# HGRN2 mixer of a hybrid encoder layer: block steps skewed by one tile, values transposed with the projections

## The chip, the cores and the metric

The kernel runs on one core of a Trainium2 chip. The core has a matmul engine (PE, with its weight loads PEld), three engines for elementwise work (DVE, ACT, GpSimd, in the profile POOL), and a sequencer, SP, that issues most DMAs. The metric is the device time of one execution in microseconds.

## What is computed

One layer of an encoder for a prompt of 1024 tokens and a sample of 64, with the same weights: a wide input projection, four token mixers side by side (A mLSTM, B forgetting attention, C HGRN2, D RG-LRU), each with a gate and a branch projection, their sum, a layer norm and a gated convolutional feed-forward. The change is in mixer C alone, 4 heads with a 128x128 state:

```python
z = hg_f.astype(F32).reshape(bsz, t_len, HG_HEADS, HG_DK)
lbh = lb.reshape(HG_HEADS, HG_DK)
hg_logf = jnp.log(jnp.maximum(lbh + (1.0 - lbh) * jax.nn.sigmoid(z), TINY))
hg_k = (1.0 - lbh) * jax.nn.sigmoid(-z)
o_hg, hg_s = hgrn2_chunkwise(jax.nn.silu(hg_q)..., hg_k, hg_i..., hg_logf, hg_s)
y_hg = head_rms_norm(o_hg, hg_norm_g).astype(x.dtype) * jax.nn.silu(hg_g)

def hgrn2_chunkwise(q, k, v, logf, s0):
    # S_t = diag(f_t) S_{t-1} + k_t v_t^T, o_t = S_t^T q_t, by blocks
    def step(s, blk):
        bcum = jnp.cumsum(fc, axis=2)
        qe = qc * jnp.exp(bcum)
        a = jnp.where(causal, jnp.einsum('bhtk,bhsk->bhts', qe, kc * jnp.exp(-bcum)), 0.0)
        o = jnp.einsum('bhts,bhsv->bhtv', a, vc) + jnp.einsum('bhtk,bhkv->bhtv', qe, s)
        b_last = bcum[:, :, -1]
        s_new = jnp.exp(b_last)[..., None] * s + jnp.einsum(
            'bhsk,bhsv->bhkv', kc * jnp.exp(b_last[:, :, None] - bcum), vc)
        return s_new, o
```

## The kernel before

Activations lie with features on partitions and the 1088 tokens along the free axis, in three chunks of 384, 384 and 320 columns. A projection (`dense`, line 311) takes for each chunk one PSUM bank and 24 matmuls: `mm3` (line 293) runs three products for each of 8 slices of the inner dimension, since weights and inputs are split into a high and a low half. The weights come by DMA as `wr`; `wh` (ACT or GpSimd, lines 259 and 261) and `wl` (DVE, line 262) are made from it a little ahead of use. `bank` hands out PSUM banks by kind, two of each: "d" for the projections (in the profile psd), "m" for transposes and scores (psm), "s" for the products (pss). Whoever takes a bank waits until the engine that empties it is done.

Mixer C runs head by head, here called unit 0 to 3. `P_C(u)` makes the projections of a head: forget gate `z`, query `qc`, value `vT`, output gate `gs`, 12 chunks in all, each evicted by ACT (`qc` and `gs` with a pass on DVE behind). `M_C(u)` does the rest in three parts:

- The front (lines 892 to 949), on whole rows of 128x1088: on ACT the absolute value of `z` (892), exponentials (893, 896) and two logarithms (897, 898) with loads of ACT's function table between; on DVE lines 899, 901, 904 and 905 and a scan (907), `dd` (911); on ACT two exponentials (913, 914); on DVE `kc` (916, it has the place of `z`) and `qc` (915); on GpSimd `qR` (947) and `kU` (949). Small passes on the block sums make `EX`, `eR`, `eU` and `eT`.
- The transposes (line 957) of `vT` and then `kU`, nine tiles each in groups of 4, 4 and 1, through an "m" bank; `vt` is copied by DVE (961), `kt` by ACT (959). There is a yield after each group.
- Nine steps, one for each tile of 128 tokens (the last has 64). `scores(t+1)`: `KX` on DVE (984), four matmuls (989), the lower triangle copied to `am` on DVE (992). `flip(t)`: a transpose of `am` (997), copied to `at` on ACT (999). `outs(t)`: the products `at` x `vt` (1009), `qR` x state (1011), `kt` x `vt` (1012), then `ot` (DVE, 1013), its square `sq` (ACT, 1015) and the new state `St` (DVE, 1018 or 1020). `tail` transposes and gates finished outputs (966 to 974).

`branch` (line 1432) weaves the generators: M_C of unit u-1 with P_C of unit u, and M_C of unit 3 with the gate projections, in the proportion of their yields, 19 to 12:

```python
for u in range(1, n):
    weave(Mg(u - 1), nM, Pg(u), nP)
weave(Mg(n - 1), nM, gates(m, range(4)), 12)
```

That gives the order in which the program is written. A scheduler then sets the final order on each engine: it moves instructions forward where their operands allow, and each engine runs its list in that order and waits at the front of it. So the front of unit u+1 lies on ACT and DVE between the last four steps of unit u.

Of the kernel before, what the change touches and what calls it, by code (L numbers as in the profile page):

```python
# [13 lines left out]
AF = mybir.ActivationFunctionType  # L14
OP = mybir.AluOpType
# [4 lines left out]
P = 128  # L20
# [14 lines left out]
HG_F, HG_I, HG_Q, HG_G = 3088, 3600, 4112, 4624  # L35
# [28 lines left out]
def tw(tt):  # L64
    return P if tt < 8 else TS
# [3 lines left out]
def trunk_kernel(ctx: ExitStack, tc: tile.TileContext, I, O, dbg=None):  # L69
    nc = tc.nc  # L70
    PE, V, S, G, SP = nc.tensor, nc.vector, nc.scalar, nc.gpsimd, nc.sync
# [239 lines left out]
    def dense(key, evict, tag="d", order=(0, 1, 2), ahead=2):  # L311
        wh, wl = wget(key, ahead)
        for c in order:
            n0, n = CH[c]
            ps = bank(tag)
            mm3(ps[:, :n], [(wh[:, k, :], wl[:, k, :], xh[c][:, k, :], xl[c][:, k, :]) for k in range(8)])
            evict(c, n0, n, ps[:, :n])
            yield
# [144 lines left out]
    pt = bank("s", 1024)  # L463
# [12 lines left out]
    def bc(c0):  # L476
        return pk[:, bcol(c0):bcol(c0) + 1]
# [273 lines left out]
    st = {}  # L751
# [96 lines left out]
    ams = []  # L848

    def blk(t, n=34):  # L850
        return t.rearrange("p (a b) -> p a b", b=32)[:, 0:n, :]

    def P_C(u):
        z = slot(s="z")
        bf = bc(HG_F + u * P)

        def ev(c, n0, n, ps):
            S.activation(z[:, n0:n0 + n], ps, AF.Identity, bias=bf)
        yield from dense(("in", HG_F + u * P), ev)

        def silu2(dst, j):
            b, bh = bc(j + u * P), bsil[j][:, u:u + 1]

            def evs(c, n0, n, ps):
                t = small([P, 384], "sil", 2)
                S.activation(t[:, :n], ps, AF.Tanh, bias=bh, scale=0.5)
                S.activation(dst[:, n0:n0 + n], ps, AF.Identity, bias=b)
                V.scalar_tensor_tensor(dst[:, n0:n0 + n], t[:, :n], 1.0, dst[:, n0:n0 + n], OP.add, OP.mult)
            return evs
        qc = slot(s="qc")  # L870
        yield from dense(("in", HG_Q + u * P), silu2(qc, HG_Q))
        vT = slot(s="vT")
        bi = bc(HG_I + u * P)

        def evv(c, n0, n, ps):
            S.activation(vT[:, n0:n0 + n], ps, AF.Identity, bias=bi)
        yield from dense(("in", HG_I + u * P), evv)
        gs = slot(s="gs")
        yield from dense(("in", HG_G + u * P), silu2(gs, HG_G))
        st["C", u] = z, qc, vT, gs  # L880

    def M_C(u):
        z, qc, vT, gs = st.pop(("C", u))
# [16 lines left out]
        kc = z  # L900
# [29 lines left out]
        EX = small([P, 9, 4, 4], "EX", 2)  # L930
# [16 lines left out]
        G.tensor_tensor(blk(qR), blk(qc), eR[:, 0:34].unsqueeze(2).to_broadcast([P, 34, 32]), OP.mult)  # L947
        kU = slot(s="kU")
        G.tensor_tensor(blk(kU), blk(kc), eU[:, 0:34].unsqueeze(2).to_broadcast([P, 34, 32]), OP.mult)
        vt, kt = slot([P, 9, P], s="vt"), slot([P, 9, P], s="kt")  # L950
        for src, dst, eng in ((vT, vt, 0), (kU, kt, 1)):
            for g0, g1 in ((0, 4), (4, 8), (8, 9)):
                pt = bank("m")
                p3 = pt.rearrange("p (a b) -> p a b", b=P)
                w = tw(g0)
                for tt in range(g0, g1):
                    PE.transpose(p3[0:w, tt - g0, :], src[:, tt * P:tt * P + w], ident)
                if eng:
                    S.activation(dst[0:w, g0:g1, :], p3[0:w, 0:g1 - g0, :], AF.Copy)
                else:  # L960
                    V.tensor_copy(dst[0:w, g0:g1, :], p3[0:w, 0:g1 - g0, :])
                yield
        ot = slot([P, 9, P], s="ot")
        ss = small([P, 9], "ss", 2)
        St = None
# [9 lines left out]
            if g1 == NT:  # L975
                yput(2, u, gs)

        def scores(tt):
            w = tw(tt)
            nb = w // 32  # L980
            t0 = tt * P
            KX = small([P, 4, 4, 32], "KX", 2)
            k4 = kc[:, t0:t0 + w].rearrange("p (j b) -> p j b", b=32)
            V.tensor_tensor(KX[:, 0:nb, 0:nb, :],
                            k4.unsqueeze(1).to_broadcast([P, nb, nb, 32]),
                            EX[:, tt, 0:nb, 0:nb].unsqueeze(3).to_broadcast([P, nb, nb, 32]), OP.mult)
            pA = bank("m")
            for i in range(nb):
                PE.matmul(pA[32 * i:32 * i + 32, 0:w], qc[:, t0 + 32 * i:t0 + 32 * i + 32],
                          KX[:, i, 0:nb, :], start=True, stop=True)  # L990
            am = ams[tt % 3]
            V.copy_predicated(am[0:w, 0:w], triL[0:w, 0:w], pA[0:w, 0:w])
            return pA, am

        def flip(tt, pA, am):
            w = tw(tt)
            PE.transpose(pA[0:w, 256:256 + w], am[0:w, 0:w], ident[0:w, 0:w])
            at = small([P, P], "at", 2)
            S.activation(at[0:w, 0:w], pA[0:w, 256:256 + w], AF.Copy)
            return at  # L1000

        def outs(tt, at, St):
            w = tw(tt)
            t0 = tt * P
            if tt == 8:
                St = small([P, P], "St", 3)
                SP.dma_start(St, I["state_hgrn_s"][0, 0, u])
            po = bank("s", 1024)
            PE.matmul(po[0:w, 0:P], at[0:w, 0:w], vt[0:w, tt, :], start=True, stop=St is None)
            if St is not None:  # L1010
                PE.matmul(po[0:w, 0:P], qR[:, t0:t0 + w], St, start=False, stop=True)
            PE.matmul(po[:, 512:640], kt[0:w, tt, :], vt[0:w, tt, :], start=True, stop=True)
            V.tensor_copy(ot[0:w, tt, :], po[0:w, 0:P])
            sq = small([P, P], "sq", 1)
            S.activation(sq[0:w], po[0:w, 0:P], AF.Square, accum_out=ss[0:w, tt:tt + 1])
            Sn = small([P, P], "St", 3)
            if St is None:
                V.tensor_copy(Sn, po[:, 512:640])
            else:
                V.scalar_tensor_tensor(Sn, St, eT[:, tt:tt + 1], po[:, 512:640], OP.mult, OP.add)  # L1020
            if tt >= 7:
                SP.dma_start(O["p_hg_s" if tt == 7 else "s_hg_s"][0, 0, u], Sn)
            if tt in (3, 7, 8):
                g0 = tt // 4 * 4
                sg = ss[0:w, g0:tt + 1]
                V.tensor_scalar(sg, sg, 1.0 / P, 1e-6, OP.mult, OP.add)
                G.tensor_tensor(sg, sg, mhalf[0:w].to_broadcast([w, tt + 1 - g0]), OP.pow)
                V.tensor_tensor(ot[0:w, g0:tt + 1, :], ot[0:w, g0:tt + 1, :],
                                sg.unsqueeze(2).to_broadcast([w, tt + 1 - g0, P]), OP.mult)
            return Sn  # L1030

        a1 = scores(0)
        for tt in range(NT):
            a0 = a1
            if tt < 8:
                a1 = scores(tt + 1)
            St = outs(tt, flip(tt, *a0), St)
            if tt == 5:
                tail(0, 4)
            yield  # L1040
# [407 lines left out]
    out_D()  # L1448
    phase("C")
    weave(chain(fox_rows(), ml_rows()), 10, P_C(0), 12)  # L1450
    branch(2, P_C, M_C, 4, 12, 19, 1)
    merge(2, 1)
    phase("B")
# [66 lines left out]
    for hf in range(2):  # L1520
# [3 lines left out]
        for i, tt in enumerate(seq):  # L1524
            w = tw(tt)
# [123 lines left out]
    pt = bank("m")  # L1649
# [46 lines left out]
    for g, grp in enumerate(TGRP):  # L1696
# [25 lines left out]
        for tt in grp:  # L1722
            w = tw(tt)
# [59 lines left out]
```

## Time and profile before

| what | us |
|---|---|
| median of 3 runs | 2140.57 (2140.0 to 2143.93) |
| the profiled execution | 2141.45 |
| span of its trace | 2139.7 |
| PE busy in the span | 2101.1 (98%) |
| window of unit 1 of mixer C | 65.5 |

The span is the trace from its first to its last instruction; the profiled execution is 1.75 us longer, and 0.9 us above the median. Busy time of PE counts matmuls whose ends are modelled, so a busy PE can still hold small gaps. "[3.32 <-DVE vt L961]" behind a row says that the engine had been idle for 3.32 us and that the copy to `vt` on line 961 released it. The rows follow after the change.

### The profile page before, as it was taken

What the parts mean: (1) busy time and instruction counts of PE and PEld (TensorE: products, weight loads), DVE (VectorE), ACT (ScalarE), POOL (GpSimd) and SP (SyncE); (2) the same over time, 40 slices, a digit from 0 to 9 for tenths busy, and PEclk for the clock granted to TensorE, in tenths of its full rate; (3) what the DMA queues carried; (4) which work ended last, traced back from release to release, by engine and by line L of the source; (5) the groups of instructions that cost most, each with busy time, mean ns of one, the idle gap of its engine ahead of it and who ended that gap; (6) DMA issues with size and microseconds to landing.
All of it is one profiled execution on the core that took longest, in us unless ns stands there. A gap on an engine that the chain in (4) does not pass through costs nothing.

```text
span 2139.7 us, 31840 instructions
## 1 busy us (share of the span) xinstructions
PE 2101.1 (98%) x13035; PEld 1955.5 (91%) x13035; DVE 1151.5 (54%) x2202; ACT 737.1 (34%) x1277; POOL 223.7 (10%) x232
## 2 busy tenths in 40 slices
PE   8999999999999999999999999999999999999998
PEld 7999999888899988889999989899889999998886
DVE  4643245665543466555332144546459766666655
ACT  3664114555321234344310123324134333334341
POOL 1100011220100322200001101000120000000112
PEclk9999999999999999999999999999999999999999
DMA  5112321111143222321432212135211222227652
GB/s 153 53 61 71 103 75 40 44 45 33 52 148 132 82 81 61 92 82 41 131 136 82 63 38 65 43 123 194 80 74 51 80 88 74 79 87 282 224 198 100
DMA packets 193229, 200.29 MB, mean 94 GB/s; under 512 B 14588, under 2 KB 165448, under 8 KB 193084
## 3 DMA queue, kind: packets, MB, share of 16 engines
q1 hardware_dynamic: 193084, 198.26, 28.8%
q8 instruction: 102, 1.67, 0.3%
q14 instruction: 43, 0.35, 0.1%
HBM read 154.80 MB, written 43.43 MB: 93 GB/s over the span
## 4 chain that ended last, share of the span: by engine, by line
PE 51%; DVE 2%; DMA 1%; ACT 0%; issue 0%; POOL 0%; SPq 0%; DVEq 0%; ACTq 0%
PE pss L368 8%; PE psd L296 7%; PE psd L298 7%; PE psd L297 7%; PE pss L1693 5%; PE psd L1693 2%; PE psm L1693 2%; PE psm L297 2%; PE psm L296 2%; PE psm L298 2%; PE pss L296 1%; PE pss L297 1%; PE pss L298 1%; PE psm L368 1%; PE psm L1330 1%; PE psm L1117 0%
## 5 line engine op out<-in xcount | busy, mean ns | idle before, releaser
L296 PE MATMUL psd<-xh,wh 128*128 128x384 f32 (+1 forms) x1920 | 643.2, 335 | 0.9 <-ACT xh L178 0.9
L298 PE MATMUL psd<-xh,wl 128*128 128x384 f32 (+1 forms) x1920 | 631.4, 329 | 0.0
L297 PE MATMUL psd<-xl,wh 128*128 128x384 f32 (+1 forms) x1920 | 630.1, 328 | 0.8 <-DVE xl L179 0.8
L262 DVE TENSOR_TENSOR wl<-wr,wh 128x1024 fp32r<-128x1024 f32 x179 | 222.7, 1248 | 327.6 <-ACT wh L261 202.5
L296 PEld LDWEIGHTS psd<-xh,wh 128*128 128x128 f32 x1920 | 362.9, 189 | 7.9 <-issue 3.0
L297 PEld LDWEIGHTS psd<-xl,wh 128*128 128x128 f32 x1920 | 361.6, 188 | 1.8 <-DVE xl L179 1.0
L298 PEld LDWEIGHTS psd<-xh,wl 128*128 128x128 f32 x1920 | 361.6, 188 | 0.4
L261 ACT ACTIVATE wh<-wr 128x1024 fp32r<-128x1024 f32 x131 | 139.0, 1061 | 376.6 <-PE psd L297 127.5
L297 PE MATMUL psm<-yl,wh 128*128 128x384 f32 (+1 forms) x384 | 125.9, 328 | 1.4 <-DVE yl L702 1.4
L298 PE MATMUL psm<-yh,wl 128*128 128x384 f32 (+1 forms) x384 | 125.7, 327 | 0.0
L296 PE MATMUL psm<-yh,wh 128*128 128x384 f32 (+1 forms) x384 | 125.0, 328 | 0.6 <-ACT yh L701 0.6
L259 POOL TENSOR_SCALAR wh<-wr 128x1024 fp32r<-128x1024 f32 x48 | 52.7, 1098 | 669.7 <-PE psd L297 266.5
L682 ACT ACTIVATE th<-psd,bhalf 128x384 f32<-128x384 f32 (+1 forms) x96 | 53.4, 558 | 156.0 <-PE psd L298 156.0
L717 DVE SCALAR_TENSOR_TENSOR th<-th,psm 128x384 f32<-128x384 f32 (+1 forms) x96 | 50.9, 531 | 104.5 <-PE psm L298 103.2
L296 PE MATMUL psd<-x1h,wh 128*128 128x320 f32 (+1 forms) x272 | 85.2, 313 | 0.6 <-DVE x1l L189 0.6
L298 PE MATMUL psd<-x1h,wl 128*128 128x320 f32 (+1 forms) x272 | 84.9, 312 | 0.0
L297 PE MATMUL psd<-x1l,wh 128*128 128x320 f32 (+1 forms) x272 | 84.7, 312 | 0.0
L1496 POOL TENSOR_TENSOR lrs<-lrs,mhalf 128x1 f32<-128x1 f32 (+1 forms) x16 | 9.8, 614 | 665.9 <-ACT hh L1640 423.9
L1180 DVE CUSTOM_DVE_ANT_0 Pt<-pss,fcb 128x128 f32<-128x128 f32 (+7 forms) x64 | 48.2, 752 | 57.6 <-PE pss L1175 57.1
L297 PEld LDWEIGHTS psm<-yl,wh 128*128 128x128 f32 x384 | 72.1, 188 | 2.1 <-DVE yl L702 2.1
L296 PEld LDWEIGHTS psm<-yh,wh 128*128 128x128 f32 x384 | 71.8, 188 | 1.5 <-ACT yh L701 1.2
L298 PEld LDWEIGHTS psm<-yh,wl 128*128 128x128 f32 x384 | 72.1, 188 | 0.0
(536 smaller groups left out, 3907.4 us busy)
## 6 DMA issues: line engine op xcount, KB each, us to landing
wr<-in_w_in_dram SPq DMA_DIRECT2D x48, 512.0 KB
wr<-in_w_ff_down_dram SPq DMA_DIRECT2D x48, 512.0 KB
wr<-in_w_mg_dram SPq DMA_DIRECT2D x32, 512.0 KB
mx_d<-th SPq DMA_DIRECT2D x24, 544.0 KB
prev<-mx_d SPq DMA_DIRECT2D x24, 544.0 KB
wr<-in_w_br_dram SPq DMA_DIRECT2D x16, 512.0 KB
wr<-in_w_ff_gate_dram SPq DMA_DIRECT2D x16, 512.0 KB
wr<-in_w_ff_up_dram SPq DMA_DIRECT2D x16, 512.0 KB
```

The lines of the kernel that those rows point to most:

```text
L259: G.tensor_scalar(h, raw, 1.0, 1.0, OP.mult, OP.mult)
L261: S.activation(h, raw, AF.Copy)
L262: V.tensor_sub(l, raw, h.bitcast(F32))
L296: PE.matmul(ps, wh, mh, start=i == 0, stop=False)
L297: PE.matmul(ps, wh, ml, start=False, stop=False)
L298: PE.matmul(ps, wl, mh, start=False, stop=i == n - 1)
L368: PE.matmul(ps, w[:, k, :], x[:, k, :], start=start and k == 0 and i == 0, stop=k == 3 and i == 2, skip_group_check=not start)
L682: S.activation(th[:, n0:n0 + n], ps, AF.Tanh, bias=b, scale=0.5)
L717: V.scalar_tensor_tensor(th[:, n0:n0 + n], th[:, n0:n0 + n], 1.0, ps[:, :n], OP.add, OP.mult)
L1180: V.tensor_tensor_reduce(Pt[:, 0:L].rearrange("p (b n) -> p b n", b=nb), ps.rearrange("p (b n) -> p b n", b=2)[:, 0:nb, 0:n], cbs[hh][:, 0 ...
L1330: PE.matmul(ps[0:w, 0:w], kt[r, t0:t0 + w], qt[r, t0:t0 + w], start=True, stop=True)
L1693: PE.matmul(ps[hf], a[:, f % 8, o:o + P], w[:, 0, sl], start=f == 0 and i == 0, stop=f == 15 and i == (2 if tt < 8 else 1))
```

## The change

In `P_C` the third generator is opened up: after the first chunk of the output gate there is a yield, the values are transposed at once by the new helper `tokens`, whose copies are made by ACT, and the two other gate chunks follow. `M_C` then gets `vt` instead of `vT`, and calls `tokens` for `kU`, with one yield instead of six around the transposes. `scores` is split into `decays` (`KX`), `scores` (the matmuls) and `lower` (the triangle), `flip` into the transpose and the copy `flipped`, `outs` into the products and `keep`. Step t holds the scores of tile t+2, the flip of t+1 (now into a spare part of the "s" bank of the products) and the products of t; the state is updated ahead of the copy of `ot` and of the square. `M_C` has 16 segments now; the weave still counts 19.

```diff
...
-        yield from dense(("in", HG_G + u * P), silu2(gs, HG_G))
-        st["C", u] = z, qc, vT, gs
+        dg = dense(("in", HG_G + u * P), silu2(gs, HG_G))
+        next(dg)
+        yield
+        vt = slot([P, 9, P], s="vt")
+        tokens(vT, vt)
+        yield from dg
+        st["C", u] = z, qc, vt, gs
+
+    def tokens(src, dst):
+
+        for g0, g1 in ((0, 4), (4, 8), (8, 9)):
+            pt = bank("m")
+            p3 = pt.rearrange("p (a b) -> p a b", b=P)
+            w = tw(g0)
+            for tt in range(g0, g1):
+                PE.transpose(p3[0:w, tt - g0, :], src[:, tt * P:tt * P + w], ident)
+            S.activation(dst[0:w, g0:g1, :], p3[0:w, 0:g1 - g0, :], AF.Copy)
...
-        vt, kt = slot([P, 9, P], s="vt"), slot([P, 9, P], s="kt")
-        for src, dst, eng in ((vT, vt, 0), (kU, kt, 1)):
...
+        kt = slot([P, 9, P], s="kt")
+        tokens(kU, kt)
+        yield
...
-            V.tensor_copy(ot[0:w, tt, :], po[0:w, 0:P])
-            sq = small([P, P], "sq", 1)
-            S.activation(sq[0:w], po[0:w, 0:P], AF.Square, accum_out=ss[0:w, tt:tt + 1])
             Sn = small([P, P], "St", 3)
             if St is None:
                 V.tensor_copy(Sn, po[:, 512:640])
             else:
                 V.scalar_tensor_tensor(Sn, St, eT[:, tt:tt + 1], po[:, 512:640], OP.mult, OP.add)
+            V.tensor_copy(ot[0:w, tt, :], po[0:w, 0:P])
+            sq = small([P, P], "sq", 1)
+            S.activation(sq[0:w], po[0:w, 0:P], AF.Square, accum_out=ss[0:w, tt:tt + 1])
...
         for tt in range(NT):
-            a0 = a1
+            if tt == 8:
+                St = small([P, P], "St", 3)
+                SP.dma_start(St, I["state_hgrn_s"][0, 0, u])
+            po = bank("s", 1024)
+            if tt < 7:
+                pA = scores(tt + 2, KX)
             if tt < 8:
-                a1 = scores(tt + 1)
-            St = outs(tt, flip(tt, *a0), St)
+                flip(tt + 1, po)
+            outs(tt, at, St, po)
+            if tt < 8:
+                at = flipped(tt + 1, po)
+            St = keep(tt, St, po)
+            if tt < 7:
+                lower(tt + 2, pA)
+            if tt < 6:
+                KX = decays(tt + 3)
...
```

What this does to the order on the engines, at three places. The first is ACT at the end of unit 0's steps and the front of unit 1; L866 and L867 evict a chunk of the output gate, L999 is `at`, L1015 `sq`, and L892 starts the front. Before:

```order
L866 ACTIVATE sil_3477<-psd_3452,bhg 128x384
L867 ACTIVATE gs_3445<-psd_3452,pk 128x384
L999 ACTIVATE at_3490<-psm_3427 128x128
L892 ACTIVATE L_3625<-z_3001 128x1088
L893 ACTIVATE L_3625<-L_3625 128x1088
L1015 ACTIVATE sq_3497,ss_3282<-pss_3492 128x128
L896 ACTIVATE en_3628<-en_3628 128x1088
L897 ACT_TABLE_LOAD
L897 ACTIVATE L_3625<-L_3625 128x1088
L866 ACT_TABLE_LOAD
L866 ACTIVATE sil_3532<-psd_3507,bhg 128x384
L867 ACTIVATE gs_3445<-psd_3507,pk 128x384
```

After (L1015 is now `at`, L1035 `sq`, L895 the copies of `vt`, L907 starts the front, L911 and L908 are its exponentials, L913 a logarithm):

```order
L866 ACTIVATE sil_3549<-psd_3524,bhg 128x384
L867 ACTIVATE gs_3517<-psd_3524,pk 128x384
L895 ACTIVATE vt_3568<-psm_3569 128x512
L1035 ACTIVATE sq_3562,ss_3191<-pss_3555 64x128
L895 ACTIVATE vt_3568<-psm_3575 128x512
L895 ACTIVATE vt_3568<-psm_3581 64x128
L907 ACTIVATE L_3642<-z_3017 128x1088
L911 ACTIVATE en_3645<-en_3645 128x1088
L908 ACTIVATE L_3642<-L_3642 128x1088
L913 ACT_TABLE_LOAD
L913 ACTIVATE en_3645<-en_3645,lb 128x1088
L866 ACT_TABLE_LOAD
```

Before, the front begins between two steps, with three chunks of the gate still to be evicted in between; after, it begins behind the three copies of `vt`, which stand behind the last `at`.

The second place is PE from the last products of unit 0 to the transposes of unit 1's `kU`. Lines 296 to 298 are the dense matmuls, most of them left out here. Before, with 24 of them between each pair of groups that "..." parts:

```order
L972 MATMUL psm_3759<-ident,ot_3281 128x64
L957 MATMUL psm_3769<-ident,vT_3248 128x128 x4
...
L957 MATMUL psm_3811<-ident,vT_3248 128x128 x4
L957 MATMUL psm_3817<-ident,vT_3248 64x128
...
L957 MATMUL psm_3849<-ident,kU_3765 128x128 x4
...
L957 MATMUL psm_3884<-ident,kU_3765 128x128 x4
L957 MATMUL psm_3890<-ident,kU_3765 64x128
L296 MATMUL psd_3900<-xh_118,wh_3639 128x384
```

After (L894 are the transposes of `tokens`, L977 those of the tail, L1024 the last product of unit 0):

```order
L1024 MATMUL pss_3555<-vt_2914,kt_3138 128x128
L894 MATMUL psm_3569<-ident,vT_3331 128x128 x4
L894 MATMUL psm_3575<-ident,vT_3331 128x128 x4
L296 MATMUL psd_3584<-xh_120,wh_3157 128x384
L297 MATMUL psd_3584<-xl_121,wh_3157 128x384
L894 MATMUL psm_3581<-ident,vT_3331 64x128
...
L977 MATMUL psm_3776<-ident,ot_3190 128x64
L296 MATMUL psd_3807<-xh_118,wh_3520 128x384
...
L297 MATMUL psd_3860<-xl_121,wh_3520 128x384
L894 MATMUL psm_3785<-ident,kU_3782 128x128 x4
L894 MATMUL psm_3791<-ident,kU_3782 128x128 x4
```

The transposes of the values moved ahead of the second gate chunk (psd_3584); between the last of them and the first of `kU` lie 144 dense matmuls, and `kU` stands behind the second matmul of the second query chunk (psd_3860), where before the whole of that chunk stood ahead of it.

The third place is PE in one step of unit 1. Before (L989 scores, L997 flip, L1009, L1011 and L1012 products):

```order
L989 MATMUL psm_4003<-KX_4001,qc_3130 32x128 x4
L997 MATMUL psm_3957<-ident,am_2988 128x128
L296 MATMUL psd_4021<-xh_122,wh_3639 128x320
L297 MATMUL psd_4021<-xl_123,wh_3639 128x320
L298 MATMUL psd_4021<-xh_122,wl_3640 128x320
L1009 MATMUL pss_4012<-vt_3767,at_4010 128x128
L1011 MATMUL pss_4012<-St_3973,qR_3763 128x128
L1012 MATMUL pss_4012<-vt_3767,kt_3768 128x128
```

After (L998 scores, L1010 flip, L1021, L1023 and L1024 products):

```order
L998 MATMUL psm_4011<-KX_3975,qc_3154 32x128 x4
L1010 MATMUL pss_4010<-ident,am_3002 128x128
L1021 MATMUL pss_4010<-vt_3568,at_3967 128x128
L1023 MATMUL pss_4010<-St_3969,qR_3780 128x128
L1024 MATMUL pss_4010<-vt_3568,kt_3784 128x128
L998 MATMUL psm_4034<-KX_4031,qc_3154 32x128 x4
```

Scores, flip and products were parted by dense matmuls and now stand in one run; the flip goes to the bank of the products.

## Rows read from the trace of the kernel before

**Rows 1.** The page: busy us of each engine, share of the span, instructions.

```profile
PE 2101.1 (98%) x13035; PEld 1955.5 (91%) x13035; DVE 1151.5 (54%) x2202; ACT 737.1 (34%) x1277; POOL 223.7 (10%) x232
```

**Rows 2.** Window of unit 1; the columns are named in the first line.

```profile
core 0: us, PE busy (x) PEld busy (x) DVE busy (x) ACT busy (x) POOL busy (x), PEclk, DMA share, GB/s
...
409.70:475.20 65.50, 63.59 (x444) 58.07 (x445) 41.84 (x76) 30.03 (x64) 11.80 (x10) 1.00 0.15 45
```

**Rows 3.** What PE waited for from 325 to 606: total us, times, longest.

```profile
PE psm L957 <- DVE vt L961: 8.3, 4, 3.3
```

**Rows 4.** What the weight loads waited for there, same columns.

```profile
PEld pss L1009 <- ACT at L999: 2.0, 11, 0.3
...
PEld pss L1009 <- issue: 1.8, 8, 0.3
```

**Rows 5.** Timeline of PE, transposes: start, duration, instruction, count, [idle before, releaser].

```profile
332.69 1.04 PE L957 MATMUL psm<-ident,vT 128*128 128x128 f32 x8
...
355.60 0.60 PE L957 MATMUL psm<-ident,kU 128*128 128x128 f32 x4
...
421.13 0.60 PE L957 MATMUL psm<-ident,kU 128*128 128x128 f32 x4
...
549.20 0.30 PE L957 MATMUL psm<-ident,vT 128*64 128x128 f32 x1 [3.32 <-DVE vt L961]
```

**Rows 6.** Timeline of PE, dense matmuls: 46 intervals between the first pair, 22 the second.

```profile
333.74 0.34 PE L297 MATMUL psd<-xl,wh 128*128 128x384 f32 x1
...
341.72 0.33 PE L298 MATMUL psd<-xh,wl 128*128 128x384 f32 x1
...
342.04 0.30 PE L297 MATMUL psd<-xl,wh 128*128 128x320 f32 x1
...
345.25 0.31 PE L298 MATMUL psd<-xh,wl 128*128 128x320 f32 x1
```

**Rows 7.** Timeline of ACT, the front of unit 0 and the start of unit 1's.

```profile
324.53 1.11 ACT L892 ACTIVATE L<-z 128x1088 f32<-128x1088 f32 x1
...
327.66 1.28 ACT L898 ACT_TABLE_LOAD   x1
...
331.94 0.58 ACT L867 ACTIVATE gs<-psd,pk 128x384 f32<-128x384 f32 x1
...
335.15 1.12 ACT L897 ACTIVATE L<-L 128x1088 f32<-128x1088 f32 x1
...
384.48 1.12 ACT L892 ACTIVATE L<-z 128x1088 f32<-128x1088 f32 x1
```

**Rows 8.** Timeline of DVE, the front of unit 0, then unit 1 at the copies.

```profile
336.30 1.29 DVE L899 SCALAR_TENSOR_TENSOR L<-z,L 128x1088 f32<-128x1088 f32 x1 [0.32 <-ACT L L897]
...
348.25 1.29 DVE L915 SCALAR_TENSOR_TENSOR qc<-qc,dd 128x1088 f32<-128x1088 f32 x1
...
349.67 1.22 DVE L262 TENSOR_TENSOR wl<-wr,wh 128x1024 fp32r<-128x1024 f32 x1
...
411.19 1.98 DVE L934 TENSOR_TENSOR EX<-EX,cmask 128x144 f32<-128x144 f32 x1
...
413.10 3.05 DVE L262 TENSOR_TENSOR wl<-wr,wh 128x1024 fp32r<-128x1024 f32 x1
```

**Rows 9.** Timeline of GpSimd, the last two passes of the front, units 0 and 1.

```profile
349.62 3.15 POOL L947 TENSOR_TENSOR qR<-qc,eR 128x1088 f32<-128x1088 f32 x1 [3.07 <-DVE qc L915]
...
352.74 2.47 POOL L949 TENSOR_TENSOR kU<-z,eU 128x1088 f32<-128x1088 f32 x1
...
410.99 2.03 POOL L947 TENSOR_TENSOR qR<-qc,eR 128x1088 f32<-128x1088 f32 x1 [0.42 <-ACT eR L941]
...
412.97 2.09 POOL L949 TENSOR_TENSOR kU<-z,eU 128x1088 f32<-128x1088 f32 x1
```

**Rows 10.** Windows in which the granted clock is of interest, same columns as Rows 2.

```profile
11.60:15.00 3.40, 1.71 (x9) 1.42 (x9) 3.02 (x8) 0.85 (x1) 0.32 (x1) 1.00 0.69 270
15.00:18.40 3.40, 3.40 (x13) 3.40 (x12) 0.00 (x0) 0.00 (x0) 0.00 (x0) 0.50 0.52 126
...
545.00:550.00 5.00, 1.68 (x12) 1.40 (x11) 4.61 (x5) 0.79 (x2) 3.00 (x2) 1.00 0.33 96
```

More of the change, by code (lines that the diff above doesn't have):

```diff
@@ L878, in P_C @@
         gs = slot(s="gs")
-        yield from dense(("in", HG_G + u * P), silu2(gs, HG_G))
-        st["C", u] = z, qc, vT, gs
+        dg = dense(("in", HG_G + u * P), silu2(gs, HG_G))
[13 more added lines that the diff above has]
+            S.activation(dst[0:w, g0:g1, :], p3[0:w, 0:g1 - g0, :], AF.Copy)
     def M_C(u):
-        z, qc, vT, gs = st.pop(("C", u))
+        z, qc, vt, gs = st.pop(("C", u))
         if not ams:
@@ L949, in M_C @@
         G.tensor_tensor(blk(kU), blk(kc), eU[:, 0:34].unsqueeze(2).to_broadcast([P, 34, 32]), OP.mult)
-        vt, kt = slot([P, 9, P], s="vt"), slot([P, 9, P], s="kt")
-        for src, dst, eng in ((vT, vt, 0), (kU, kt, 1)):
[L952 to L962, printed above, removed]
+        kt = slot([P, 9, P], s="kt")
+        tokens(kU, kt)
+        yield
         ot = slot([P, 9, P], s="ot")
@@ L976, in tail, with decays, scores @@
                 yput(2, u, gs)
-        def scores(tt):
+        def decays(tt):
+            nb = tw(tt) // 32
+            KX = small([P, 4, 4, 32], "KX", 2)
+            k4 = kc[:, tt * P:tt * P + tw(tt)].rearrange("p (j b) -> p j b", b=32)
+            V.tensor_tensor(KX[:, 0:nb, 0:nb, :],
+                            k4.unsqueeze(1).to_broadcast([P, nb, nb, 32]),
+                            EX[:, tt, 0:nb, 0:nb].unsqueeze(3).to_broadcast([P, nb, nb, 32]), OP.mult)
+            return KX
+        def scores(tt, KX):
             w = tw(tt)
@@ L981, in scores @@
             t0 = tt * P
[L982 to L986, printed above, removed]
             pA = bank("m")
@@ L990, in scores, with lower, flip, flipped @@
                           KX[:, i, 0:nb, :], start=True, stop=True)
+            return pA
+        def lower(tt, pA):
+            w = tw(tt)
             am = ams[tt % 3]
             V.copy_predicated(am[0:w, 0:w], triL[0:w, 0:w], pA[0:w, 0:w])
-            return pA, am
-        def flip(tt, pA, am):
+        def flip(tt, po):
             w = tw(tt)
-            PE.transpose(pA[0:w, 256:256 + w], am[0:w, 0:w], ident[0:w, 0:w])
+            PE.transpose(po[0:w, 256:256 + w], ams[tt % 3][0:w, 0:w], ident[0:w, 0:w])
+        def flipped(tt, po):
+            w = tw(tt)
             at = small([P, P], "at", 2)
-            S.activation(at[0:w, 0:w], pA[0:w, 256:256 + w], AF.Copy)
+            S.activation(at[0:w, 0:w], po[0:w, 256:256 + w], AF.Copy)
             return at
-        def outs(tt, at, St):
+        def outs(tt, at, St, po):
             w = tw(tt)
             t0 = tt * P
[L1005 to L1008, printed above, removed]
             PE.matmul(po[0:w, 0:P], at[0:w, 0:w], vt[0:w, tt, :], start=True, stop=St is None)
@@ L1012, in outs, with keep @@
             PE.matmul(po[:, 512:640], kt[0:w, tt, :], vt[0:w, tt, :], start=True, stop=True)
-            V.tensor_copy(ot[0:w, tt, :], po[0:w, 0:P])
-            sq = small([P, P], "sq", 1)
-            S.activation(sq[0:w], po[0:w, 0:P], AF.Square, accum_out=ss[0:w, tt:tt + 1])
+        def keep(tt, St, po):
+            w = tw(tt)
             Sn = small([P, P], "St", 3)
@@ L1030, in outs @@
             return Sn
-        a1 = scores(0)
-        for tt in range(NT):
-            a0 = a1
-            if tt < 8:
-                a1 = scores(tt + 1)
-            St = outs(tt, flip(tt, *a0), St)
+        KX = decays(0)
+        lower(0, scores(0, KX))
+        KX = decays(1)
+        yield
+        pf = bank("m")
+        flip(0, pf)
+        at = flipped(0, pf)
+        lower(1, scores(1, KX))
+        KX = decays(2)
+        yield
+        for tt in range(NT):
+            if tt == 8:
[4 more added lines that the diff above has]
+                pA = scores(tt + 2, KX)
+            if tt < 8:
+                flip(tt + 1, po)
[7 more added lines that the diff above has]
+                KX = decays(tt + 3)
             if tt == 5:
```

## The prediction

> **What bounds the kernel now.** I read the page first. The matmul engine is busy for 2101.1 of the 2139.7 us span [rows 1], so the time is matmul work plus the gaps in it, and a change that leaves the matmuls alone can only move some 38 us of gaps. The change leaves every dense matmul and every small product in place (11631 rows of the PE order become 11632), so I then looked at the HGRN stretches alone. They run from 332.7 to 604 us. Unit 1, the window of one middle unit, is 65.5 us long with 63.59 us of busy PE [rows 2]. DVE is busy 42 and ACT 30 of these 65 us: neither is the bound on average, but each can be late at one point. Where PE waits in them is the third view: 8.3 us in four waits, one a unit, at the last transpose of the values, which needs the bank that the DVE copy `vt` is to empty [rows 3]. The weight loads of the step products add 2.0 us for `at`, in 11 waits, and 1.8 us of "issue" at the same place [rows 4].
>
> **What is removed.** The value transposes now follow the first gate chunk, their copies are on ACT, which is free there, and DVE no longer has the copy behind `EX`, a 3.05 us `wl` and `KX` [rows 8]. The four waits (the one of 3.32 us is the longest, [rows 5]) go: 8.3 us. In the steps, `at` of tile t+1 is made one step ahead and the state update stands ahead of the copy of `ot` and the square, so the 2.0 us go too, and perhaps the 1.8. The scores, the flip and the products of a step now stand in one run on PE with dense work behind, as the third piece of the order shows; they cost what they did. Bounds: 8.3 (if the step waits come back at another product) to 12.1. I take **-11 us**, near the upper end, because the skew gives both `at` and the state a whole step.
>
> **What is moved.** That is the term that decides. The transposes of `kU` open the products of a unit, and `kU` is the end of a long chain: absolute value, exponentials and logarithms of the gate on ACT, five passes and a scan on DVE, two exponentials on ACT, `kc` and `qc` on DVE, `qR` and `kU` on GpSimd. Before, in units 1 to 3, this front is woven into the last four steps of the unit ahead: it starts at 384.48 [rows 7], `kU` ends at 415.06 [rows 9], and PE asks for it at 421.13 [rows 5], 6 us later. After, by the order of ACT, the front starts only behind the three `vt` copies, which come after the last step; and by the order of PE the transposes of `kU` stand two matmuls into the second q chunk, where before they stood behind the whole of it, with the value transposes ahead. So the chain starts later and is wanted earlier.
>
> How long is it when nothing of a previous unit is in its way? Unit 0 of before shows just this: same ACT order (absolute value, two exponentials, table load, logarithm, table load, evictions of the second and third gate chunk, table load, second logarithm). It starts at 324.53 and the second logarithm starts at 335.15 and takes 1.12 [rows 7], 11.7 us after the start. DVE follows at 336.30 and begins `qc` at 348.25 [rows 8]; `qR` runs from 349.62 for 3.15 us, `kU` from 352.74 for 2.47 [rows 9]. End: 355.21, that is 30.7 us. PE came at 355.60 [rows 5], 0.4 us after: in unit 0 the cover was just enough, with three gate and state groups, the value transposes and the whole second q chunk in it. The lower bound of the chain takes 2.03 and 2.09 us for the two GpSimd passes, as unit 1 has them [rows 9], which takes away 1.5, and some 0.9 us because the small DVE passes can stand elsewhere: 28.3 us.
>
> Now PE from the end of the last step's products, for units 1 and 2 (time 0). A 384-column matmul takes 7.98 us/46 = 0.1735 us, so a chunk of 24 takes 4.16; a 320-column one 3.21 us/22 = 0.146, a chunk 3.52 [rows 6]. Nine 128-column transposes are 1.1 (eight took 1.04, [rows 5]). Second gate chunk to 5.25, third to 8.77. The first z chunk needs the bank of the second gate chunk; ACT evicts that only behind the second table load, at 2.1 + 8.1 = 10.2 us (absolute value, two exponentials, 1.28 us load, logarithm, load, and two evictions of 0.58 each; where the front starts at 2.1, behind an eviction pair and the three copies): **1.5 us** of a new wait. Then z to 14.5, 18.6, tail transposes 0.5, third z 22.6, q 26.9, two matmuls 27.3. `kU` is there at 2.1 + 28.3 = 30.4 to 2.1 + 30.7 = 32.8: **3.1 to 5.5 us** of a second wait. Together 4.6 to 7.0 a unit.
>
> Unit 0, the same way: the transposes of `kU` stand 16 matmuls into the q chunk, the chain starts at 2.7 but its first logarithm is the one that the DVE passes wait for, and `en` comes 2.6 us earlier than above; PE is there at 25.7 (with a bank wait of 0.8), `kU` at 28.4 to 30.8: 3.5 to 5.9. Unit 3 has gate work instead of the q chunk; the `wl` of its DVE stands ahead of the scan and waits for ACT's `wh`, which I put at half a microsecond: 5.4 to 7.0.
>
> Sum: 3.5 + 2 x 4.6 + 5.4 = 18.1 to 5.9 + 2 x 7.0 + 7.0 = 26.9; I take **+22 us**, the middle, since the GpSimd passes took the longer time in one of the two places shown and the shorter one in the other. Copies moved from DVE to ACT are 12 of 0.7 us or less, between evictions that PE doesn't wait for; the store of a state and the load of the next on SP stay in their order. I put both at nothing; if ACT's copies delay an `at`, it is 0.3 us a time, as now [rows 4].
>
> Net +11: the profiled execution (2141.45 us, span 2139.7) would become 2152.4, and the median 2140.57 about **2151.5 us**. The slower case's own range is 18.1 - 12.1 = +6 to 26.9 - 8.3 = +18.6: 2146.5 to 2159.
>
> **A rule beside the row.** `qR` took 3.15 us beside a `wl` of 1.22, and in unit 1 2.03 us beside an `EX` pass of 1.98 us and a `wl` of 3.05 [rows 8, 9]: where one was short, the other was long. The Trainium skill, "SBUF — State Buffer", section "Who interferes with whom", says that DVE and GpSimd share one pair of ports and that who issues first holds it for its whole instruction. By that rule, which the rows agree with, the longer GpSimd times are those in which a DVE pass went first; with `wl` always first the sum would be its upper end, with `qR` always first its lower.
>
> **The rivals.** (1) Faster: the front hides anyway. It would have to take 25 us or less from its start, or start in step 7. Then the 11 us go and only bank waits (1.5 + 1.5 + 0.8 + 1.5 = 5.3, or none) come: 2129.5 to 2135. For it: idle ACT and DVE, and the place of `kU` in the order, in mid chunk, which looks like a place at which it was reckoned to be ready. Against it: 30.7 us in unit 0 with nothing of HGRN beside. 14%. (2) No change: the wait for `kU` is 1 to 1.5 us a unit, the chain near 26 us: +4 to +6 and +5.3 of bank waits against -11, about 2140 with 4 us to either side. 16%. (3) Slower still: PE's clock falls in the waits. The granted clock was 0.50 (1.2 GHz) from 15.0 to 18.4, behind a stretch in which PE was busy for 1.71 of 3.40 us; 3.4 us at that level cost 1.7. Against it: PE had only 1.68 busy us of 5.00 from 545 to 550 and was granted 1.00 throughout [rows 10]. One fall a unit gives 4 x 1.7 = +6.8: 2158. 8%. The Trainium skill, "TensorE: Matmul & The Clock Gate", "Part 1: The HAM clock gate (the "warmup" mystery)", says that an idle array falls back to its lower clock; by that rule the time would be that 2158, and only the first of the two stretches agrees. (4) The skew does nothing (the step waits return at other products): only the 8.3 go, 2154; it lies in the main case's range.
>
> **How the numbers follow.** Main case, slower by the late front: 62%; with (3) 70% for slower by over 0.2%, which is 4.3 us and about what a measurement of this kernel can tell from no change. Within 0.2%: 16%. Faster: 14%. The range leaves out most of (1) and what lies beyond the clock case: 2135 to 2159.
>
> **What would show it.** Right: a PE wait at the first transpose of `kU`, released by GpSimd, of 3 to 5.5 us, once a unit; a wait of about 1.5 us at the first z chunk, released by the gate eviction on ACT; no wait for `vt`; hardly one for `at`; windows of a middle unit of about 68 us. Wrong: `kU` ends ahead of PE's arrival, most likely since the front starts earlier than the end of the steps, or is under 26 us.

## The result and the profile after

The changed kernel takes 2161.27 us (median of 4 runs, 2159.35 to 2162.43) against 2141.24 for the kernel before in the same comparison: a ratio of 1.0087, 95% interval 1.0075 to 1.0099. The profiled execution has a span of 2160.1 us, 20.4 more than before. The forecast, 2151.5, had the sign and the place of the loss; the time lies 2 us beyond the end of its range.

PE's busy time on the page (the row that answers to [rows 1]; same columns) and the windows of two middle units, from one value transpose to the next (they answer to [rows 2], same columns):

```profile
PE 2109.0 (98%) x13035; PEld 1963.6 (91%) x13035; DVE 1149.4 (53%) x2190; ACT 744.1 (34%) x1289; POOL 223.0 (10%) x232
```
```profile
395.60:466.60 71.00, 65.00 (x446) 59.35 (x445) 40.16 (x74) 32.06 (x67) 11.76 (x9) 0.98 0.14 41
...
466.60:536.90 70.30, 64.33 (x442) 59.08 (x441) 39.77 (x74) 33.00 (x69) 9.64 (x7) 0.98 0.13 41
```

A middle unit takes 71.0 and 70.3 us where it took 65.5. Two things are new in the rows: some 6 us without a matmul instead of 1.9, and a mean clock of 0.98 where it was 1.00; with it goes a *longer* busy time of PE (2109.0 against 2101.1) for the same 13035 matmuls.

What PE waited for in mixer C (answers to [rows 3]: total us, times, longest), and three of these waits in PE's timeline (start, duration, instruction, [idle before, releaser]):

```profile
PE psm L894 <- POOL kU L964: 18.5, 4, 5.2
...
PE psd L296 <- ACT gs L867: 3.5, 4, 1.5
```
```profile
406.07 0.41 PE L296 MATMUL psd<-xh,wh 128*128 128x384 f32 x1 [1.48 <-ACT gs L867]
...
428.03 1.97 PE L894 MATMUL psm<-ident,kU 128*128 128x128 f32 x8 [4.52 <-POOL kU L964]
...
568.30 1.97 PE L894 MATMUL psm<-ident,kU 128*128 128x128 f32 x8 [5.25 <-POOL kU L964]
```

No matmul waits for `vt` any more, and no weight load for `at`. In their place stand four waits for `kU` of 4.2 to 5.3 us and four for the gate eviction on ACT, of 1.5 us in units 1 and 2 and of 0.3 us in units 0 and 3. The front of unit 1 on ACT and on GpSimd (answers to [rows 7, 9]) shows why:

```profile
397.69 1.11 ACT L907 ACTIVATE L<-z 128x1088 f32<-128x1088 f32 x1
...
405.36 0.57 ACT L867 ACTIVATE gs<-psd,pk 128x384 f32<-128x384 f32 x1
...
408.08 1.11 ACT L912 ACTIVATE L<-L 128x1088 f32<-128x1088 f32 x1
```
```profile
423.00 2.02 POOL L962 TENSOR_TENSOR qR<-qc,eR 128x1088 f32<-128x1088 f32 x1 [3.34 <-DVE qc L930]
...
424.98 3.00 POOL L964 TENSOR_TENSOR kU<-z,eU 128x1088 f32<-128x1088 f32 x1
```

The front starts at 397.69, behind the copies of `vt`; the second logarithm ends 11.5 us later and `kU` ends at 427.98, 30.3 us after the start. PE's wait of 4.52 us ends at 428.03 with the transposes of `kU`.

The front starts later than it did by the steps, but not by the dense work: 2046 dense matmuls lie ahead of its start, where it was 2044. The chain is no longer either, 30.3 us against 30.6 (384.48 to 415.06 [rows 7, 9]). What shrank is PE's work between the start of the front and the transposes of `kU`: 36.7 us before (384.48 to 421.13 [rows 5, 7]), with 164 dense matmuls and four steps in it, and 25.8 us now, with 140 and none.

What follows is the third cost, in windows with the columns of [rows 2]:

```profile
354.50:359.30 4.80, 4.80 (x21) 4.21 (x25) 0.97 (x1) 1.54 (x4) 0.00 (x0) 0.50 0.39 109
...
424.00:427.50 3.50, 0.00 (x0) 0.00 (x0) 3.50 (x2) 0.00 (x0) 3.50 (x2) 1.00 0.45 167
...
428.00:431.00 3.00, 2.97 (x12) 2.97 (x13) 1.13 (x2) 1.19 (x2) 0.00 (x0) 0.50 0.46 138
...
499.40:502.70 3.30, 3.30 (x14) 3.30 (x13) 0.70 (x2) 1.20 (x2) 0.00 (x0) 0.50 0.22 67
...
568.20:574.40 6.20, 6.10 (x29) 4.70 (x30) 2.08 (x4) 2.05 (x4) 0.05 (x1) 0.50 0.00 0
```

PE does nothing from 424.0 to 427.5; from 428.0 to 431.0, when it works again, the granted clock is 0.50, which is the lower of the two levels, 1.2 GHz. It fell at the end of all four waits for `kU` or just behind them. At 0.50 the same work takes about twice as long: eight transposes of `kU` took 1.97 us here, and 1.04 is what eight transposes took at 1.00 [rows 5]. Summed over windows of 1 us in mixer C, PE was busy for 17.5 us at 0.50; half of that, **8.8 us**, is lost (an estimate from these rows). So the 20.4 us of span are 18.5 + 3.5 us of waits and 8.8 of clock, less 10.4. This last number is not measured; it is what is left over, and a little of it is not the change's doing. The traces already differ by 1.2 us ahead of mixer C's first front, at the transposes of `mli`, and by 22.4 us at its last transpose. The rows, first before, then after:

```profile
318.50 0.69 PE L653 MATMUL psm<-ident,mli 4*128 4x4 f32 x9
...
604.00 0.28 PE L972 MATMUL psm<-ident,ot 64*128 64x64 f32 x1
```
```profile
319.73 0.68 PE L653 MATMUL psm<-ident,mli 4*128 4x4 f32 x9
...
626.35 0.27 PE L977 MATMUL psm<-ident,ot 64*128 64x64 f32 x1
```

Between these points the change lost 21.1 us, so by the same sum it saved 9.7 us there.

### The profile page after: what moved, and what is told of

Read it like the earlier page. It is cut to its first block, busy times and chain, and to the rows that moved or that the text cites. A ratio compares the mean times of both kernels' runs of the same rounds, so it can differ in the third digit from the quotient of the medians.

```text
span 2160.1 us, 31893 instructions
## 1 busy us (share of the span) xinstructions
PE 2109.0 (98%) x13035; PEld 1963.6 (91%) x13035; DVE 1149.4 (53%) x2190; ACT 744.1 (34%) x1289; POOL 223.0 (10%) x232
## 4 chain that ended last, share of the span: by engine, by line
PE 50%; DVE 2%; DMA 1%; POOL 0%; issue 0%; ACT 0%; DVEq 0%; SPq 0%; ACTq 0%; POOLq 0%
PE pss L368 8%; PE psd L296 7%; PE psd L298 7%; PE psd L297 7%; PE pss L1729 5%; PE psm L296 2%; PE psd L1729 2%; PE psm L1729 2%; PE psm L297 2%; PE psm L298 2%; PE pss L296 1%; PE pss L297 1%; PE pss L298 1%; PE psm L368 1%; PE psm L1366 1%; PE psm L1153 0%
```

## The experiments

Theory L (late front): the change's two parts save what they were reckoned to, but the front of a unit now starts behind the last step and `kU` is wanted too early; the waits, and the clock that falls with them, are the whole loss. Rival S: the steps packed on PE cost it. Rival V: the three more copies on ACT cost it. Ratios are to the kernel before, run beside each experiment.

**e1, values alone.** The new `P_C` and `tokens` with the old steps:

```diff
-        for tt in range(NT):
-            ...
-                pA = scores(tt + 2, KX)
-                flip(tt + 1, po)
-            outs(tt, at, St, po)
+        a1 = scores(0)
+        for tt in range(NT):
+            a0 = a1
+            if tt < 8:
+                a1 = scores(tt + 1)
+            St = outs(tt, flip(tt, *a0), St)
```

> The values are transposed with the projections and copied by ACT, as in the changed kernel; the steps are the old ones (scores of t+1, flip and products of t, copy of ot and square ahead of the state). Theory L (the front starts too late and kU is wanted too early): by the order, the front still starts behind the copies of vt and kU stands 142 dense matmuls behind the last value transpose (144 in the changed kernel), so the waits for kU of 4 to 5 us a unit and the fallen clock behind them are here too; only the 2 us of step waits for at come back: 2160 to 2165 us. Rival S (the steps packed on PE are what costs): only the 8.3 us of waits for the copy of vt are gone, 2131 to 2134 us. Rival V (three more copies on ACT are what costs): 2160 too, but without a wait for kU.

Measured: 2161.77 us, 1.0081 (1.0066 to 1.0096). PE's waits, columns as above:

```profile
PE psm L894 <- POOL kU L964: 17.2, 4, 4.5
...
PE psd L296 <- ACT gs L867: 4.2, 4, 1.3
```

The waits for `kU` and the loss are all here with the old steps: S is out. V, in the form in which the copies cost something without a wait for `kU`, is out as well.

**e2, skew alone.** The new steps; `vT` handed to `M_C` and transposed there, copied by DVE, as before.

```diff
-        vt = slot([P, 9, P], s="vt")
-        tokens(vT, vt)
-        yield from dg
-        st["C", u] = z, qc, vt, gs
+        st["C", u] = z, qc, vT, gs
...
-        kt = slot([P, 9, P], s="kt")
-        tokens(kU, kt)
-        yield
+        vt, kt = slot([P, 9, P], s="vt"), slot([P, 9, P], s="kt")
+        for src, dst, eng in ((vT, vt, 0), (kU, kt, 1)):
+            ...
```

> The steps are skewed as in the changed kernel; the values are transposed in the second part of a unit and copied by DVE, as before. By the order, the front starts between the last steps of the unit ahead again, and kU stands behind the value transposes. Theory L: no wait for kU, waits for vt of about 8 us as before, hardly any for at: 2136 to 2141 us, granted clock 1.00 in all units. Rival S: the step packing costs what the changed kernel lost, 2152 to 2161 us. Rival V: as L.

Measured: 2142.47 us, 0.9994 (0.9983 to 1.0004), 1.5 us above the range of L. The wait and, behind the wait of unit 1, a window:

```profile
PE psm L967 <- DVE vt L971: 8.0, 3, 3.2
```
```profile
419.00:422.00 3.00, 3.00 (x10) 3.00 (x11) 1.76 (x4) 0.00 (x0) 0.00 (x0) 0.50 0.65 175
```

The wait for `kU` is gone and that for `vt` is back. What I had not expected is the 0.50: two waits of 3.2 us for `vt` were followed by the lower clock, 6.4 busy us in all, 3.2 lost. In the trace of before, the longest wait was of 3.32 us [rows 5] and the clock stayed [rows 10]. Without those 3.2 us the span of 2141.5 would be 2138.3, 1.4 below before. That is an estimate of what the skew is worth, from one execution of each kernel; the ratio itself is not clear of no change.

**e3, work in the wait.** 20 transposes of `qR` ahead of those of `kU`:

```diff
         kt = slot([P, 9, P], s="kt")
+        pw = bank("m")
+        for _ in range(20):
+            PE.transpose(pw[:, 0:P], qR[:, 0:P], ident)
         tokens(kU, kt)
```

> The changed kernel with 20 more transposes of one tile of qR ahead of those of kU, 2.2 us of work a unit whose result nobody reads. By the order they come 5 dense matmuls (0.9 us) earlier than kU stood. The one wait of 4 to 5 us for kU becomes two of about 2 (for qR) and 1 us (for kU). If idle PE is what drops the clock, the granted clock stays at 1.00 behind kU, and the time is that of the changed kernel less about 8 us of half clock plus 4 x 0.9 us: 2155 to 2158 us. If the clock falls for another reason (the packed products of the steps), it falls here as well: 2161 to 2165 us.

Measured: 2162.08 us, 1.0082 (1.0067 to 1.0097).

```profile
PE psm L968 <- POOL qR L962: 11.8, 4, 4.1
...
PE psm L894 <- POOL kU L964: 1.1, 2, 0.6
...
PE pss L1026 <- DMA St<-in_state_hgrn_s_dram: 1.7, 2, 1.5
```
```profile
394.00:396.00 2.00, 0.57 (x4) 0.19 (x2) 0.69 (x1) 1.05 (x2) 0.04 (x1) 1.00 0.05 8
...
398.00:400.00 2.00, 2.00 (x9) 1.85 (x8) 0.94 (x3) 1.74 (x6) 0.54 (x1) 0.50 0.11 33
```

A miss in the time, and half an answer. In units 1 and 2, with waits of 2.69 and 2.43 us for `qR` and 0.56 for `kU`, the clock did not fall; in unit 0, with 2.64, and in unit 3, with 4.06, it did, and it fell at another place, behind a step that waited 1.5 us for the state from DRAM, which the window from 394 shows with 0.57 busy us of 2.00. The added transposes, some 2.2 us a unit at full clock, ate what the shorter waits gave. That idle PE and the lower clock go together is shown: in the twelve traces here every fall in mixer C stands at a wait of 1.5 us or more, or just behind it. How much idle it takes is not, and I leave it open.

**e4, e7, e8: bring `kU` forward.** GpSimd makes `qR` first and `kU` second, though `kU` does not need `qc`. e8 swaps the two, e7 adds a yield ahead of `tokens(kU, kt)`, e4 does both.

```diff
-        qR = slot(s="qR")
-        G.tensor_tensor(blk(qR), blk(qc), eR[:, 0:34]...)
         kU = slot(s="kU")
         G.tensor_tensor(blk(kU), blk(kc), eU[:, 0:34]...)
+        qR = slot(s="qR")
+        G.tensor_tensor(blk(qR), blk(qc), eR[:, 0:34]...)
+        yield
         kt = slot([P, 9, P], s="kt")
         tokens(kU, kt)
```

> The changed kernel with the two GpSimd passes in the other order (kU, then qR) and one yield ahead of the transposes of kU, which puts them at the same place in the second q chunk but behind one more step product group. kU no longer waits for qc and qR: it is there some 4 us earlier. Theory L: the waits for kU shrink to less than 1 us a unit, the clock stays at 1.00, and of the new waits only the 3.5 us for the gate eviction on ACT stay: 2133 to 2139 us. Rivals S and V: the time stays within 4 us of the changed kernel's 2161.

> Half of experiment e4: one yield ahead of the transposes of kU, the order of the two GpSimd passes as in the changed kernel. By the order kU stands one dense matmul and one group of products later than in the changed kernel, 0.7 us. Theory L: the wait for kU stays at about 4 us a unit, and the clock falls behind it: 2153 to 2160 us. If the yield was what helped in e4: 2139 to 2145 us.

> The other half of e4: kU ahead of qR on GpSimd, no yield added. kU is there some 4 us earlier, but the scheduler also puts its transposes 12 dense matmuls (2.1 us) earlier. Theory L: the wait is 2 to 3 us a unit instead of 4.7, and as no wait is over 3 us the clock stays at 1.00, which is worth another 8.8 us: 2141 to 2147 us. If the clock falls behind such a wait as well: 2148 to 2154 us.

Measured: e4 2140.77 us, 0.9985 (0.9976 to 0.9994); e7 2154.07, 1.0044 (1.0029 to 1.0059); e8 2155.00, 1.0049 (1.0031 to 1.0067). PE's waits of e4, of e7 and of e8, in this order, and unit 1 of e4, the start of the front and GpSimd:

```profile
PE psm L894 <- POOL kU L962: 6.0, 3, 2.0
PE psm L999 <- DVE KX L988: 0.4, 2, 0.2
PE psd L296 <- ACT gs L867: 0.3, 1, 0.3
```
```profile
PE psm L894 <- POOL kU L964: 15.2, 4, 4.7
PE psd L296 <- ACT gs L867: 0.3, 1, 0.3
```
```profile
PE psm L894 <- POOL kU L962: 13.6, 4, 3.6
PE psd L296 <- ACT gs L867: 3.5, 4, 1.5
```
```profile
389.80 1.11 ACT L907 ACTIVATE L<-z 128x1088 f32<-128x1088 f32 x1
...
414.02 2.93 POOL L962 TENSOR_TENSOR kU<-z,eU 128x1088 f32<-128x1088 f32 x1 [2.46 <-DVE z L931]
...
416.91 2.09 POOL L964 TENSOR_TENSOR qR<-qc,eR 128x1088 f32<-128x1088 f32 x1
```

e7 was as expected: 15.2 us of waits for `kU`, 2.8 to 4.7 each, and the lower clock behind all four; it gained 3.2 us at the gate wait (3.5 to 0.3) and 3.3 us at `kU`. e8 missed, above both of its ranges: the scheduler moved `kU` to an earlier place as soon as it was ready earlier, 13.6 us of waits stayed (3.2 to 3.6 a unit, where I had said 2 to 3), and the clock fell behind each of them. The 3 us that I had put as a limit there is none: in unit 0 of e7 a wait of 2.81 us was followed by 0.50.

Only both together bring the waits to 2 us, and at that size the clock stayed at 1.00 in mixer C. e4 missed as well, by 1.8 us: three waits of 2.0 us for `kU` stayed where I had said less than 1, and of the gate waits 0.3 us where I had said 3.5. In unit 1 the chain took 27.2 us, 3.1 less than in the changed kernel and not 4, for the pass that now comes first took 2.93 us.

Between e8 and e4 the waits for `kU` and the gate differ by 17.1 - 6.3 = 10.8 us, and e8 lost another 6.6 us to the clock (13.2 busy us at 0.50): 17.4. e4 has 2.1 us of its own, 0.4 for `KX` and 1.7 for 3.4 us at 0.50 from 24.3, ahead of mixer C. That leaves 15.3, where the spans differ by 15.6 us (2153.3 and 2137.7): waits and clock are all but the whole difference.

**e6, steps spread.** e4's swap without its yield, and the weave told of 12 segments:

```diff
-    branch(2, P_C, M_C, 4, 12, 19, 1)
+    branch(2, P_C, M_C, 4, 12, 12, 1)
```

> The changed kernel with kU ahead of qR on GpSimd and the weave of mixer C counting 12 segments instead of 19, which by the order leaves the last three steps of a unit behind the value transposes of the next and puts kU 155 to 165 dense matmuls behind them (144 in the changed kernel). The chain's end is some 4 us earlier and is wanted 2 to 5 us later, but the front has the last steps beside it again. Theory L: no wait for kU, clock 1.00: 2130 to 2137 us. If the front is drawn out by the steps beside it by over 5 us, a wait of 1 to 3 us a unit stays: 2138 to 2146 us. Rivals S and V: 2155 to 2165 us.

Measured: 2139.55 us, 0.9974 (0.9965 to 0.9983). Its trace has 4.5 us of waits for `kU`, the longest 2.4, and one fall of the clock. It is the second case of the expectation: with steps beside it the chain of unit 1 took 35.1 us, 8 more than in e8. PE came 34.1 us after its start, so a wait of 1.0 was left.

**e5, e9, e10: leave the order alone, move the copies.** e9 is the kernel before with the copies of `vt` on ACT; e5 is e2 with the same edit; e10 is e5 with `kU` ahead of `qR`.

```diff
-                if eng:
-                    S.activation(dst[0:w, g0:g1, :], p3[0:w, 0:g1 - g0, :], AF.Copy)
-                else:
-                    V.tensor_copy(dst[0:w, g0:g1, :], p3[0:w, 0:g1 - g0, :])
+                S.activation(dst[0:w, g0:g1, :], p3[0:w, 0:g1 - g0, :], AF.Copy)
```

> Experiment e2 (steps skewed, values transposed in the second part of a unit as before) with the copies of vt on ACT instead of DVE. By the order the front of the next unit starts between the last steps, as before, and the copies come behind its exponentials. Theory L: no wait for kU, none for vt, the clock stays at 1.00; e2 loses its 8.0 us of waits and the 3.2 us that the half clock cost it (6.4 busy us at 0.50): 2129 to 2134 us. Rival V (three more copies on ACT are what costs): no gain over e2, 2139 to 2143 us.

> The kernel before with one edit: vt copied by ACT instead of DVE. Theory L: the 8.3 us of waits for vt go as in e5, the step waits for at of some 2 us stay, the clock is at 1.00: 0.9955 to 0.9975 of before, 2 us above e5. If the skew is what made e5 fast: within 0.2% of before.

> Experiment e5 with kU ahead of qR on GpSimd. In e5 only unit 0 still waited for kU (1.2 us), behind a qR of 4.36 us; kU would be there 4 us earlier. Theory L: this 1.2 us goes, nothing else changes: 0 to 2 us less than e5, 0.993 to 0.9946 of before. If qR, now last, comes late for the second step: up to 3 us more than e5.

Measured: e9 2135.44 us, 0.9968 (0.9956 to 0.9980); e5 2132.64, 0.9946 (0.9931 to 0.9961); e10 **2130.04**, 0.9943 (0.9931 to 0.9956). PE's waits in e9 and e5, the weight loads' waits for `at` in e9 (answers to [rows 4]) and in e10, and a window over the four units of e10:

```profile
PE psm L957 <- ACT vt L958: 2.0, 2, 1.1
...
PE psm L957 <- POOL kU L949: 1.2, 1, 1.2
...
PEld pss L1006 <- ACT at L996: 2.0, 11, 0.2
```
```profile
PE psm L967 <- POOL kU L959: 1.2, 1, 1.2
...
PE psm L967 <- ACT vt L968: 0.9, 1, 0.9
...
PEld pss L1012 <- ACT at L1017: 0.8, 3, 0.3
```
```profile
330.00:600.00 270.00, 269.85 (x1876) 248.11 (x1875) 160.67 (x294) 129.42 (x276) 44.38 (x31) 1.00 0.16 49
```

All three lie in the ranges that L gave, though waits of 1.2 us for `kU` and of 0.9 and 2.0 for `vt` stayed in e5 and e9, where I had expected none. The copy on ACT alone is worth 0.32%, 6.9 us; of the 8.3 us of waits for `vt` it leaves 2.0, and the 1.2 for `kU` come on top. What the skew adds is not clear of the noise: the spans of e5 and e9 are 2131.3 and 2133.0, 1.7 us apart, and the ratios 0.0022 with intervals that overlap. With the values left in `M_C` the front of the next unit starts between the last steps, as it did before: in unit 1 of e5 PE comes 36.7 us after the front starts, and the chain takes 34.1. In e10 it takes 32.3, PE is busy for 269.85 of 270 us, and no wait for `vt` or `kU` is left. That kernel is 0.57% faster than before and 1.4% faster than the changed one.

## Why the prediction was right, and where it was not

- **What bounds the kernel**: right. The time moved by the gaps in PE's work, as the page said; only that some of these gaps also made the work behind them slower.
- **Removed, -11 us**: near. The waits for `vt` and `at` are not in the trace, and 9.7 us (mixer C) to 10.4 (the whole span) is what the sum leaves for them; nothing measures this term alone.
- **"The chain starts later and is wanted earlier"**: the second half is what counts. By the dense work the front starts where it did; PE's work between its start and `kU` fell from 36.7 to 25.8 us.
- **The wait for `kU`**: right in mechanism, place and size. The chain took 30.3 us from the start of the front in unit 1 (28.3 to 30.7 were the bounds), and PE had nothing left to do 25.8 us after that start (25.2 forecast). The four waits sum to 18.5 us.
- **The wait at the z chunk**: right, 1.48 and 1.46 us in units 1 and 2 (1.5 forecast), but 0.26 us in units 0 (0.8) and 3 (1.5). Both waits together: 22.0 us, and 22 was the sum's term. A middle unit took 71.0 and 70.3 us, not 68; 1.5 and 1.7 us of that are clock.
- **What failed is the clock, rival (3).** The sum has no term for it. I gave it 8%, since PE had 1.68 busy us of 5.00 from 545 to 550 and kept its clock [rows 10], and priced it at 6.8 us. One stretch that kept its clock was taken for the rule, while the row beside it, in which 1.71 us of 3.40 were followed by 0.50, spoke the other way. The clock fell with all four waits and cost 8.8 us: 1.5 and 1.7 us in units 1 and 2, 2.5 and 3.1 in units 0 and 3. With 8.8 in the prediction's own sum, 22 + 8.8 - 11 = 19.8, the time is 2160.4 us, where 2161.27 was measured. The range ended at 2159 because the case of the falling clock stood in it with too low a price.
- **The page cited there** (the Trainium skill, "TensorE: Matmul & The Clock Gate", "Part 1: The HAM clock gate (the "warmup" mystery)") says that an idle array falls back to its lower clock. By that rule the four falls were to be expected, and these runs agree: it fell with 4 of 4 waits for `kU` here, again with 4 of 4 in e7 and in e8 (2.8 to 4.7 us), and with none in e4 (2.0 us). They do not show how long PE must be idle: waits of 1.5 to 3.3 us went either way.
- **The rival "faster"** leaned on the place of `kU` in the order, in mid chunk, as a sign that it would be ready there. It was not: a place in the scheduler's order is its own reckoning, 4.2 to 5.3 us off here.
- **The rule on the shared ports** (the Trainium skill, "SBUF — State Buffer", "Who interferes with whom") only set where in 28.3 to 30.7 us the chain would end. That page of the Trainium skill has the hold for a whole instruction at DVE's two-port modes; of a DVE pass with two inputs in SBUF, as `wl`, it says that it contends with GpSimd's reads. The trace agrees with a hold here too. In unit 1 `qR` started at 423.00, ahead of `wl`, and took 2.02 us; `wl` took 2.85, where it had taken 1.22 [rows 8]. `kU` started while that `wl` ran and took 3.00. In the prediction's own pair, though, the longer `qR` starts 0.05 us ahead of its `wl` [rows 8, 9], so `wl` was not plainly first there; a short pass of DVE was still running. That pass, before, and the `wl` of unit 1, after:

```profile
349.46 0.30 DVE L934 TENSOR_TENSOR EX<-EX,cmask 128x144 f32<-128x144 f32 x1
```
```profile
423.25 2.85 DVE L262 TENSOR_TENSOR wl<-wr,wh 128x1024 fp32r<-128x1024 f32 x1
```

## What to carry to other kernels

When work is moved ahead in a stream, look at what it takes out from between the start of a chain on the *other* engines and its use: here nine transposes and three copies a unit were cheap, but a chain of 30 us was left with 25.8 us of matmul work to hide behind, where it had 36.7. Where the wait was one engine's late copy, the cheaper edit was to give the copy to another engine and leave the order alone (-0.3%; with the skew and `kU` ahead of `qR`, -0.57%). And a wait on the matmul engine should be priced with what follows it: in this kernel 18.5 us of long waits cost another 8.8 us in clock.

## What the runs showed of the hardware

- The granted clock of PE dropped to 0.50 with each of the four waits for `kU` here (4.2 to 5.3 us), with all of those in e1 (3.9 to 4.5), e7 (2.8 to 4.7) and e8 (3.2 to 3.6), with two of 3.2 us in e2, two in e3 (2.64 and 4.06) and one of 2.38 in e6, and once behind 1.5 us (e3); it stayed at 1.00 with one of 3.32 us before, with 2.69 and 2.43 in e3 and with three of 2.0 in e4. The length of one wait does not settle it between these.
- The same wait in the same code can go either way. Ahead of mixer C, where the kernels are alike, every trace has a wait of 1.50 us on PE. In the changed kernel, e1 and e4 it was followed by 3.4 us at 0.50, in the nine others by 1.00. The wait and the stretch behind it, before, then in the changed kernel:

```profile
22.86 0.88 PE L177 MATMUL pss<-ident,xt 128*128 128x128 f32 x6 [1.50 <-DVE xl L179]
```
```profile
24.90:28.20 3.30, 3.30 (x21) 3.30 (x20) 2.46 (x14) 2.76 (x7) 0.86 (x1) 1.00 0.47 47
```
```profile
23.03 0.88 PE L177 MATMUL pss<-ident,xt 128*128 128x128 f32 x6 [1.50 <-DVE xl L179]
```
```profile
24.90:28.20 3.30, 3.30 (x13) 3.30 (x12) 2.33 (x13) 2.93 (x7) 1.05 (x1) 0.50 0.58 70
```

- So one trace is one draw. Of 42 runs of the kernel before beside the experiments, 16 had a mean clock of 0.995 or 0.996 and a median of 2146.5 us; eight had 0.998 or 0.999 and 2141.1. Its trace shown here is one of the latter.
- In the changed kernel PE ran at that level for 3.0 to 6.1 busy us each time before the clock rose, so a unit paid 1.5 to 3.1 us: a wait of 4.5 us cost 1.5 in unit 1, one of 5.3 us 3.1 in unit 3.
- A GpSimd pass over 128x1088 took 2.02 to 4.36 us for the same work. `qR` took 2.02 in unit 1 of the changed kernel, where the `wl` beside it took 2.85; the longest, `qR` in unit 0 of e5, had a `wl` of 1.22 and two `KX` of 0.68 us on DVE beside it:

```profile
349.10 4.36 POOL L957 TENSOR_TENSOR qR<-qc,eR 128x1088 f32<-128x1088 f32 x1 [3.07 <-DVE qc L925]
```
